# Attention on one core: adaLN columns spread over all its units, VectorE in written order, and a head group's sum of squares taken two units later

## The chip, the core and the metric

The kernel runs on one core of a Trainium2 chip. The metric is device time in microseconds (us) of one execution. The engines are TensorE (PE, with its weight loads PEld), VectorE (DVE), ScalarE (ACT), GpSimd (POOL) and SyncE (SP), which issues the loads from HBM.

## What is computed

One encoder layer on 256 tokens of width 2048, all in float32: a gated feed-forward half step, sixteen heads of attention, and a second half step. Nine vectors of the vector `c` (adaLN: shift, scale and gate of each of the three parts) modulate it.

```python
mod = jax.nn.silu(c) @ w_ada[l] + b_ada[l]
sh1, sc1, gt1, sh2, sc2, gt2, sh3, sc3, gt3 = jnp.split(mod, N_MOD, axis=-1)
f = swiglu(modulate(rms_norm(h, g_ffn1[l]), sh1, sc1), w1_gate[l], w1_up[l], w1_down[l])
h = h + 0.5 * gt1[:, None, :] * f
nrm = modulate(rms_norm(h, g_mix[l]), sh2, sc2)
qkv = nrm @ w_qkv[l]
...
o_na = rms_norm(o_na.reshape(B, S, D_NA), g_out_na[l])
o_dil = rms_norm(o_dil.reshape(B, S, D_DIL), g_out_dil[l])
mix = jnp.concatenate([o_na, o_dil], axis=-1) @ w_o[l]
h = h + gt2[:, None, :] * mix
f = swiglu(modulate(rms_norm(h, g_ffn2[l]), sh3, sc3), w2_gate[l], w2_up[l], w2_down[l])
h = h + 0.5 * gt3[:, None, :] * f
```

Heads 0 to 7 (neighbourhood attention) and heads 8 to 15 (dilated attention) each have a norm of their own over the eight heads' outputs, `o_na` and `o_dil`: that is where a head group's sum of squares is needed.

## The kernel before

**Weights as a stream.** All weights come in chunks of 128 x 1024 float32 (512 KB), loaded by SP into five `raw` buffers (`rw`). Each chunk is split in two: ACT casts it to a rounded `hiw` (L144), DVE subtracts to get the rest, `low` (L147). PE multiplies with both. There are `LOB = 4` buffers of each half, and chunks are prepared `AHEAD = 3` chunks ahead, so the cast for chunk u + 4 refills the buffer that the matmuls of chunk u read.

**Units and slots.** In attention one chunk is one *unit*: 96 of them make q, k and v (four groups of heads, 24 units each, eight units for each of v, k and q; L606 and L609), and 32 more, units 96 to 127, make the output projection (L643 and L648; 16 for heads 0 to 7, then 16 for heads 8 to 15). `at(u, fn)` puts small work into *slot* u, which the program writes behind unit u's matmuls. The heads' attention goes into the slots of the units that follow their q, k and v, by the table `PLAN`: transposes of q and k (`pT`) and their split (`th`, `tl`); scores (`psc`), bias and maximum (`sc`, `mx`), exponential, reciprocal and scaling (`sm`, `sc`); transposes of the weights (`pP`) and their split (`ph`, `pl`); the product with v (`po`), and last `d_ew`: ACT and DVE write both halves of the head's output (`ox`), ACT squares `po` (`sq`, L193), and DVE adds the square to the group's sum (`sqa`, L183). With the eighth head, PE adds up over partitions with two matmuls against ones (`pstat`, L206 and L207), in that head's own slot. From `pstat` comes `rsr`, which every unit of the output projection needs in its update `fin`, one slot after its matmuls: an ACT copy `wt`, and on DVE L632, L633 and L634, which adds to the residual `h`. In the second half the update's square goes to a further sum for the next norm.

**adaLN columns.** A column of `w_ada` is 1 MB (`ra`), reduced against `c` by one DVE instruction and its accumulator read (both L127). Columns that are not due yet are taken from a list `bg` at a rate: each chunk prepared earns `ws.rate` of a column. In attention the list holds the 22 columns of the next feed-forward part (vectors 6 and 7).

**What sets the order.** Every engine runs its list from the front. A scheduler makes the lists, except for engines under `manual_schedule`, which keep the written order. Through units 8 to 121 that is PE alone (`MANUAL`); ahead of that and behind it PE and DVE (`STARTUP`). `keep_in_program_order` (the set `pinned`) holds single instructions in written order.

Of the kernel before, what the change touches and what calls it, by code (L numbers as in the profile page):

```python
# [12 lines left out]
ALU = mybir.AluOpType  # L13
# [3 lines left out]
S = 256  # L17
D = 2048
KT = D // P
# [15 lines left out]
TAIL = 6  # L35
# [5 lines left out]
RA = 0.475  # L41
RB = 0.33
RBD = 0.45
RQ = 0.35
RF = 0.1
AHEAD = 3
RAWB = 5
ARA = 2
ARX = 1
LOB = 4  # L50
MANUAL = {mybir.EngineType.PE}
STARTUP = {mybir.EngineType.PE, mybir.EngineType.DVE}
# [12 lines left out]
def build(tc, a):  # L65
    nc = tc.nc
    with ExitStack() as ctx:
# [17 lines left out]
        def bank(nm):  # L85
            return pools["p"].tile([P, 512], F32, tag="b", name=nm)
# [3 lines left out]
        ones = cp.tile([P, P], F32, name="ones")  # L90
# [83 lines left out]
        class Stat:  # L174
# [11 lines left out]
            def add(self, t, last_dve=True, late=False):  # L186
                self.fold()
                sq = sp.tile([P, S], F32, tag="sq", name="sq")
                self.n += 1
                if self.n == self.total and last_dve:  # L190
                    nc.vector.tensor_tensor(sq, t, t, ALU.mult)
                else:
                    nc.scalar.activation(sq, t, AF.Square)  # L193
                n, total = self.n, self.total
                if n == 1:
                    self.first = sq
                elif n == 2:
                    self.acc = sp.tile([P, S], F32, tag="sqa", bufs=1, name="sqa")
                    nc.vector.tensor_tensor(self.acc, self.first, sq, ALU.add)
                elif n < total:  # L200
                    self.late = sq
                    if not late:
                        self.fold()
                else:
                    self.ps = bank("pstat")[:, :S]
                    nc.tensor.matmul(self.ps, ones, self.acc, start=True, stop=False)  # L206
                    nc.tensor.matmul(self.ps, ones, sq, start=False, stop=True)  # L207

            def rstd(self, n, tag="rs"):
                return rstd_from(self.ps, n, S, tag)  # L210

        def norm_pair(ks, r, jsh, jsc):

            sh, gs = mods[jsh], mods[jsc]
            ts = []
            for k in ks:
                ts.append(sp.tile([P, S], F32, tag="nt", name="nt"))
                nc.vector.scalar_tensor_tensor(ts[-1], h[k], gs[:, k : k + 1], r, ALU.mult, ALU.mult)
                nc.scalar.activation(nx[k][:, 0, :], ts[-1], AF.Identity, bias=sh[:, k : k + 1])  # L219
            for k, t in zip(ks, ts):  # L220
                nc.vector.scalar_tensor_tensor(  # L221
                    nx[k][:, 1, :], t, sh[:, k : k + 1], nx[k][:, 0, :].bitcast(F32), ALU.add, ALU.subtract)
# [13 lines left out]
        pinned = set()  # L236

        def bg_add(ids, then=None):

            ids = list(ids)  # L240
            bg.extend((i, then if i == ids[-1] else None) for i in ids)
# [17 lines left out]
        def bg_until(left):  # L259

            while len(bg) + len(pend) > left:
                if bg:
                    bg_step()
                else:
                    bg_use()
# [194 lines left out]
        for q in range(4):  # L460
            for i in range(2):
                sq = hp.tile([P, 2, S], F32, tag="hid", name="sq1")
# [13 lines left out]
        with tc.manual_schedule(engines=STARTUP):  # L476
# [3 lines left out]
            for k in range(K1):  # L480
                ws.fetch(2 * k + 2)
                bg_until((KT - 1 - k) * 2)
                for j in range(2):
                    w = ws.whole()
                    for b in range(8):
                        f, q = 4 * j + b // 2, b % 2
                        nc.tensor.matmul(pa[f][:, q, :], w[:, b * P : (b + 1) * P], full[k],
                                         start=k == 0 and q == 0, stop=k == K1 - 1 and q == 1,
# [41 lines left out]
        with tc.tile_pool(name="att", bufs=2) as ap_, tc.tile_pool(name="atc", bufs=1) as ac:  # L530
# [16 lines left out]
            ost = [Stat(8), Stat(8)]  # L547
# [6 lines left out]
            def at(u, fn):  # L554
                slots.setdefault(u, []).append(fn)
# [97 lines left out]
            def head(g, i, a0, b0, c0, d0):  # L653
                hd = g * 4 + i
# [61 lines left out]
                def d_ew():  # L716
                    po = s_["po"]
                    go = vec[:, GO + hd : GO + hd + 1]
                    nc.scalar.activation(ox[hd][:, 0, :], po, AF.Copy, scale=go)
                    nc.vector.scalar_tensor_tensor(  # L720
                        ox[hd][:, 1, :], po, go, ox[hd][:, 0, :].bitcast(F32), ALU.mult, ALU.subtract)
                    ost[hd // 8].add(po, False)

                def fetch():
                    s_["bias"] = na_bias(hd) if g < 2 else lnc

                at(max(0, a0 - 2), fetch)
                for u, fn in ((a0, a_pe), (a0 + 1, a_ew), (b0, b_pe), (b0 + 1, b_ew1), (b0 + 2, b_ew2),
                              (c0, c_pe), (c0 + 1, c_ew), (d0, d_pe), (d0 + (0 if d0 == LAST else 1), d_ew)):
                    at(u, fn)  # L730

            last = [j * KT + k for k in range(K2, KT) for j in (7, 6)]
            pinned.update(last[:ARA + 1])
            bg_add(last)
            units = []
            for g in range(4):
# [4 lines left out]
            LAST = len(units) + KT - 1  # L741
            END = len(units) + 2 * KT - 1
# [3 lines left out]
            def run(us):  # L746
                for u in us:
                    if u % 24 == 0 and u <= 72:
                        plan = PLAN if u < 72 else PLAN_L
                        for i in range(4):  # L750
                            head(u // 24, i, *(u + 24 + x for x in plan[i]))
                    if u == END - 2 * TAIL:
                        bg_until(0)
                    units[u](*ws.chunk())
                    if u < 7:
                        norm_pair((2 * u + 2, 2 * u + 3), r2, 3, 4)
                    for f in slots.pop(u, []):
                        f()

            run(range(8))  # L760
            order.close()
            ws.pace(RQ)
            with tc.manual_schedule(engines=MANUAL):
                run(range(8, END - TAIL))
            order.enter_context(tc.manual_schedule(engines=STARTUP))
            run(range(END - TAIL, len(units)))
            for u in sorted(slots):
                for f in slots[u]:
# [5 lines left out]
            last = [8 * KT + k for k in range(KT)]  # L774
# [113 lines left out]
def _program():  # L888
    import concourse.bacc as _bacc

    nc = _bacc.Bacc("TRN2", target_bir_lowering=False, num_devices=1, dynamic_dma_scratch_size=1024)
    aps = {k: nc.dram_tensor(f"in_{k}_dram", s, F32, kind="ExternalInput").ap() for k, s in _SHAPES.items()}
    aps["out"] = nc.dram_tensor("out_0_dram", (KT, P, S), F32, kind="ExternalOutput").ap()
    with tile.TileContext(nc) as tc:
        build(tc, aps)
    return nc
# [10 lines left out]
```

## Time and profile before

| | us |
|---|---|
| median of 3 runs (1944.61 to 1949.75) | 1945.46 |
| the profiled execution | 1942.14 |
| its span, first to last instruction | 1940.4 |
| mean granted PE clock | 0.994 |
| first q/k/v matmul to first output-projection matmul | 782.5 to 1083.6 |
| last output-projection matmul to first matmul of the next part | 1189.1 to 1198.0 |

The profile is of one execution. "Busy" is the time in which an engine works; a wait names the engine and the line whose end released it. The clock is given as a share of full speed. Attention takes about 415 us of the span; what stands ahead of it and behind it is not touched by the change.

### The profile page before, as it was taken

Reading aid. Unit: us, or ns where it says so; the run is one execution under the profiler, and the core shown is the slowest. Engines: PE = TensorE matmul, PEld = TensorE weight load, DVE = VectorE, ACT = ScalarE, POOL = GpSimd, SP = SyncE. Lnnn points to the kernel's source line nnn. Section 1 sums busy time; section 2 is a strip of 40 time slices with the busy share of each in tenths; the row PEclk is TensorE's granted clock in tenths of the full one; section 3 lists DMA queues with packets and bytes.
Section 4 is the critical chain, followed back from the end, with each engine's and each line's share of the span. In section 5 each row is a group of like instructions: output and inputs, shape, how many; then the busy total and the mean of one; then the engine's idle time right before and its main releaser. Section 6 shows DMA issues by size and latency. Waiting matters only on the chain.

```text
span 1940.4 us, 27380 instructions
## 1 busy us (share of the span) xinstructions
PE 1899.4 (98%) x10504; PEld 1648.6 (85%) x10504; DVE 1523.3 (79%) x2055; ACT 907.5 (47%) x1332; POOL 0.7 (0%) x6
## 2 busy tenths in 40 slices
PE   7999999999999999899999998999999999999999
PEld 6878888888888888688888887888888888888888
DVE  7898999999878889699986898668865555555665
ACT  2444544443334454445555565544444433334442
POOL 0000000000000000000000000000000000000000
PEclk9999999999999999999999999999999999999999
DMA  9998888899989898598865544668865666666664
GB/s 392 386 340 303 315 305 309 305 329 395 356 302 345 310 321 311 171 326 324 318 222 165 163 142 146 192 213 318 323 206 186 188 190 186 190 189 187 191 194 134
DMA packets 120083, 503.98 MB, mean 260 GB/s; under 512 B 13328, under 2 KB 15632, under 8 KB 101520
## 3 DMA queue, kind: packets, MB, share of 16 engines
q1 hardware_dynamic: 119952, 502.24, 74.5%
q8 instruction: 82, 1.34, 0.3%
q14 instruction: 49, 0.40, 0.1%
HBM read 500.09 MB, written 2.10 MB: 259 GB/s over the span
## 4 chain that ended last, share of the span: by engine, by line
PE 53%; DVE 4%; issue 1%; ACT 1%; DMA 0%; SPq 0%; ACTq 0%; DVEq 0%
PE pb L338 17%; PE pb L340 9%; PE pd L338 8%; PE pd L340 4%; PE pqq L606 3%; PE pqk L606 3%; PE pqv L606 3%; DVE low L147 2%; PE pqq L609 1%; PE pqk L609 1%; PE pqv L609 1%; PE pso L643 1%; DVE wt L633 1%; PE psc L153 0%; PE po L153 0%
## 5 line engine op out<-in xcount | busy, mean ns | idle before, releaser
L144 ACT CAST hiw<-rw 128x1024 fp32r<-128x1024 f32 x644 | 675.0, 1051 | 793.8 <-PE pd L338 233.7
L147 DVE TENSOR_TENSOR low<-rw,hiw 128x1024 fp32r<-128x1024 f32 x644 | 783.4, 1221 | 293.9 <-ACT hiw L144 286.8
L338 PE MATMUL pb<-nx,hiw 128*128 128x512 f32 x2432 | 610.5, 393 | 4.1 <-DVE nx L221 4.1
L338 PEld LDWEIGHTS pb<-nx,hiw 128*128 128x128 f32 x2432 | 438.4, 189 | 83.0 <-issue 4.4
L340 PEld LDWEIGHTS pb<-nx,low 128*128 128x128 f32 x2432 | 331.7, 190 | 24.5 <-DVE low L147 0.8
L338 PE MATMUL pd<-hd,hiw 128*128 128x512 f32 x1384 | 346.7, 392 | 0.0
L340 PE MATMUL pb<-nx,low 128*128 128x256 f32 x2432 | 339.2, 282 | 0.4 <-DVE low L147 0.4
L338 PEld LDWEIGHTS pd<-hd,hiw 128*128 128x128 f32 x1384 | 248.9, 189 | 44.4
L127 DVE CUSTOM_DVE_ANT_0 ra<-ra,cb,vec 128x2048 f32<-128x2048 f32 x109 | 255.7, 2346 | 11.4 <-DMA ra<-in_w_ada_dram 11.3
L340 PEld LDWEIGHTS pd<-hd,low 128*128 128x128 f32 x1408 | 191.7, 190 | 13.6 <-DVE low L147 0.3
L340 PE MATMUL pd<-hd,low 128*128 128x256 f32 x1408 | 196.5, 282 | 0.0
L402 DVE SCALAR_TENSOR_TENSOR h<-pd,m,h 128x256 f32<-128x256 f32 x126 | 59.5, 481 | 59.4 <-PE pd L340 59.0
L127 DVE CUSTOM_DVE_ANT_0 rx<-rx,cb,vec 128x2048 f32<-128x2048 f32 x35 | 82.1, 2346 | 2.1 <-DMA rx<-in_w_ada_dram 2.1
L338 PE MATMUL pa<-nx,hiw 128*128 128x512 f32 x288 | 72.6, 394 | 6.2 <-ACT hiw L144 6.2
L606 PE MATMUL pqv<-hiw,nx 128*128 128x512 f32 x256 | 66.7, 403 | 5.4 <-ACT nx L219 5.4
L338 PEld LDWEIGHTS pa<-nx,hiw 128*128 128x128 f32 x288 | 51.7, 189 | 16.7 <-ACT hiw L144 7.4
L606 PE MATMUL pqk<-hiw,nx 128*128 128x512 f32 x256 | 65.4, 396 | 0.3 <-ACT hiw L144 0.3
L606 PE MATMUL pqq<-hiw,nx 128*128 128x512 f32 x256 | 64.6, 394 | 0.0
L643 PE MATMUL pso<-ox,hiw 128*128 128x512 f32 x248 | 64.2, 402 | 0.0
L606 PEld LDWEIGHTS pqv<-hiw,nx 128*128 128x128 f32 x256 | 48.3, 193 | 17.8 <-ACT nx L219 7.9
L606 PEld LDWEIGHTS pqk<-hiw,nx 128*128 128x128 f32 x256 | 46.4, 188 | 9.5 <-ACT hiw L144 0.7
L606 PEld LDWEIGHTS pqq<-hiw,nx 128*128 128x128 f32 x256 | 46.8, 188 | 9.1
(143 smaller groups left out, 1370.9 us busy)
## 6 DMA issues: line engine op xcount, KB each, us to landing
ra<-in_w_ada_dram SPq DMA_DIRECT2D x109, 1024.0 KB, 7.3
rw<-in_w_b_dram SPq DMA_DIRECT2D x200, 512.0 KB, 4.4
rw<-in_w_d_dram SPq DMA_DIRECT2D x128, 512.0 KB, 4.3
rw<-in_w_c_dram SPq DMA_DIRECT2D x96, 512.0 KB, 3.6
rw<-in_w_qkv_dram SPq DMA_DIRECT2D x96, 512.0 KB, 4.4
rx<-in_w_ada_dram SPq DMA_DIRECT2D x35, 1024.0 KB, 7.1
rw<-in_w_e_dram SPq DMA_DIRECT2D x48, 512.0 KB, 4.6
rw<-in_w_a_dram SPq DMA_DIRECT2D x44, 512.0 KB, 5.3
```

The lines of the kernel that those rows point to most:

```text
L127: dot = nc.vector.tensor_tensor_reduce(out=raw, in0=raw, in1=cb, scale=1.0, scalar=vec[:, BA + i : BA + i + 1], op0=ALU.mult, op1=ALU.add, ...
L144: cast = nc.scalar.copy(hi, raw)
L147: nc.vector.tensor_tensor(lo, raw, hi.bitcast(F32), ALU.subtract)
L338: nc.tensor.matmul(out, w, r, start=first, stop=False)
L340: nc.tensor.matmul(out[:, :S], lo[:, b * P : (b + 1) * P], r[:, 0, :], start=False, stop=last)
L402: nc.vector.scalar_tensor_tensor(h[d], part_, gate(d), h[d], ALU.mult, ALU.add)
L606: nc.tensor.matmul(ps[t], nx[k][:, i, t * P : (t + 1) * P], whi[:, kk * 512 : (kk + 1) * 512], start=k + i == 0, stop=False)
L609: nc.tensor.matmul(ps[t], nx[k][:, 0, t * P : (t + 1) * P], wlo[:, kk * 512 : (kk + 1) * 512], start=False, stop=k == KT - 1)
L633: nc.vector.scalar_tensor_tensor(t, t if u < END else ps[:, :S], gt2[:, d : d + 1], rows[b], ALU.mult, ALU.mult)
L643: nc.tensor.matmul(ps, w, o, start=kk == 0, stop=False)
```

## The change

Five edits, four of them in attention. `RQ`, the rate of the columns in attention, goes from 0.35 to 0.26 of a column a chunk. All 22 columns are pinned, not the first three. DVE joins PE under written order in units 8 to 121. What is left of the columns is used up at unit 95 (`LAST - KT`, ahead of the output projection) and not at unit 115. For the two head groups (`last_dve` false) the last square is added on DVE like the others (L209), and PE's total is one matmul, in a new function `total_up`, two units after the eighth head's `po`.

```diff
-RQ = 0.35
+RQ = 0.26
...
-                else:
+                elif last_dve:
                     self.ps = bank("pstat")[:, :S]
                     nc.tensor.matmul(self.ps, ones, self.acc, start=True, stop=False)
                     nc.tensor.matmul(self.ps, ones, sq, start=False, stop=True)
+                else:
+                    nc.vector.tensor_tensor(self.acc, self.acc, sq, ALU.add)
+
+            def total_up(self):
+                self.ps = bank("pstat")[:, :S]
+                nc.tensor.matmul(self.ps, ones, self.acc, start=True, stop=True)
...
                     ost[hd // 8].add(po, False)
+                    if hd % 8 == 7:
+                        at(d0 + 2, ost[hd // 8].total_up)
...
-            pinned.update(last[:ARA + 1])
+            pinned.update(last)
...
-                    if u == END - 2 * TAIL:
+                    if u == LAST - KT:
                         bg_until(0)
...
-            with tc.manual_schedule(engines=MANUAL):
+            with tc.manual_schedule(engines=STARTUP):
                 run(range(8, END - TAIL))
```

**What moves: ACT, units 109 to 111.** Heads 12 to 15 finish here. `sq_10517` is the square of head 13, `hiw_10593` (before: `hiw_10595`) the cast of the chunk for unit 115, and `pso_10456` and `pso_10498` are units 109 and 110. Before:

```order
L719 ACTIVATE ox13_7103<-po_10473,vec_76 128x256
L631 COPY wt_10532<-pso_10456 128x256
L144 CAST hiw_10539<-rw_10537 128x1024
L719 ACTIVATE ox14_7104<-po_10520,vec_76 128x256
L156 CAST ph_10565<-pP_10527 128x512
L631 COPY wt_10583<-pso_10498 128x256
L193 ACTIVATE sq_10517<-po_10473 128x256
L144 CAST hiw_10595<-rw_10593 128x1024
```

The same place on ACT after the change, begun a little earlier, with the cast for unit 113 (`hiw_10494`) and head 12's square (`sq_10426`):

```order
L144 CAST hiw_10494<-rw_10492 128x1024
L193 ACTIVATE sq_10426<-po_10374 128x256
L725 ACTIVATE ox13_7103<-po_10473,vec_76 128x256
L690 ACTIVATE sc_10438,sm_10442<-sc_10438,mx_10440 128x256 x2
L144 CAST hiw_10539<-rw_10537 128x1024
L637 COPY wt_10532<-pso_10456 128x256
L725 ACTIVATE ox14_7104<-po_10520,vec_76 128x256
L156 CAST ph_10565<-pP_10527 128x512
L637 COPY wt_10581<-pso_10498 128x256
L144 CAST hiw_10593<-rw_10591 128x1024
L193 ACTIVATE sq_10517<-po_10473 128x256
```

Head 13's square has moved from ahead of the cast for unit 115 to behind it, and head 12's stands behind the cast for unit 113. ACT's order is the scheduler's in both kernels.

**DVE, the same place.** `pl_10566` is the rest of head 15's weights, which PE's `po` of head 15 needs. Before:

```order
L720 SCALAR_TENSOR_TENSOR ox13_7103<-po_10473,vec_76,ox13_7103 128x256
L632 TENSOR_TENSOR wt_10532<-wt_10532,pso_10456 128x256
L147 TENSOR_TENSOR low_10540<-rw_10537,hiw_10539 128x1024
L183 TENSOR_TENSOR sqa_9651<-sqa_9651,sq_10517 128x256
L633 SCALAR_TENSOR_TENSOR wt_10532<-wt_10532,m5_83,rsr_9972 128x256
L720 SCALAR_TENSOR_TENSOR ox14_7104<-po_10520,vec_76,ox14_7104 128x256
L634 TENSOR_TENSOR h3_93<-h3_93,wt_10532 128x256
L157 TENSOR_TENSOR pl_10566<-pP_10527,ph_10565 128x512
L183 TENSOR_TENSOR sqa_9651<-sqa_9651,sq_10562 128x256
```

After, DVE:

```order
L726 SCALAR_TENSOR_TENSOR ox13_7103<-po_10473,vec_76,ox13_7103 128x256
L183 TENSOR_TENSOR sqa_9646<-sqa_9646,sq_10517 128x256
L638 TENSOR_TENSOR wt_10532<-wt_10532,pso_10456 128x256
L639 SCALAR_TENSOR_TENSOR wt_10532<-wt_10532,m5_83,rsr_9972 128x256
L640 TENSOR_TENSOR h3_93<-h3_93,wt_10532 128x256
L147 TENSOR_TENSOR low_10540<-rw_10537,hiw_10539 128x1024
L726 SCALAR_TENSOR_TENSOR ox14_7104<-po_10520,vec_76,ox14_7104 128x256
L183 TENSOR_TENSOR sqa_9646<-sqa_9646,sq_10562 128x256
L157 TENSOR_TENSOR pl_10566<-pP_10527,ph_10565 128x512
```

The addition of head 13's square stands right behind `ox13` now, ahead of the update of unit 109 and the split for unit 114, and head 14's stands ahead of `pl_10566` instead of behind it.

**DVE and ACT, unit 44.** `ox2` belongs to head 2; `sm_8280` and `sc_8276` (before: `sm_8291`, `sc_8287`) are head 3's weights, which PE transposes (`pP`) behind unit 45. DVE before:

```order
L720 SCALAR_TENSOR_TENSOR ox2_7092<-po_8280,vec_76,ox2_7092 128x256
L690 RECIPROCAL sm_8291<-sm_8291 128x2
L127 ISA ra107_8406,m6_84<-ra107_8406,cb_98,vec_76 128x2048
L127 ISA m6_84 128x1
L183 TENSOR_TENSOR sqa_8161<-sqa_8161,sq_8319 128x256
L695 TENSOR_SCALAR sc_8287<-sc_8287,sm_8291 128x256 x2
```

DVE after:

```order
L726 SCALAR_TENSOR_TENSOR ox2_7092<-po_8269,vec_76,ox2_7092 128x256
L183 TENSOR_TENSOR sqa_8151<-sqa_8151,sq_8308 128x256
L696 RECIPROCAL sm_8280<-sm_8280 128x2
L701 TENSOR_SCALAR sc_8276<-sc_8276,sm_8280 128x256 x2
L147 TENSOR_TENSOR low_8317<-rw_8314,hiw_8316 128x1024
```

ACT after, where `hiw_8339` is the cast for unit 49:

```order
L725 ACTIVATE ox2_7092<-po_8269,vec_76 128x256
L144 CAST hiw_8316<-rw_8314 128x1024
L690 ACTIVATE sc_8276,sm_8280<-sc_8276,mx_8278 128x256 x2
L144 CAST hiw_8339<-rw_8337 128x1024
L193 ACTIVATE sq_8308<-po_8269 128x256
```

The column that stood between `sm` and `sc` is gone from this place, `sqa` has moved ahead of both, and head 2's square stands behind the cast for unit 49.

On SP the loads of the columns stand behind every fourth chunk's load instead of every second or third, the last three among those of the output projection. On PE nothing moves but `pstat`.

## The prediction

> **What bounds the kernel now.** I read the busy shares first, then the chain that ended last, then what TensorE (PE) waited for inside attention (770 to 1200 us), and the stages last. The page gives busy time by engine, and the chain's shares:
>
> ```profile
> PE 1899.4 (98%) x10504; PEld 1648.6 (85%) x10504; DVE 1523.3 (79%) x2055; ACT 907.5 (47%) x1332; POOL 0.7 (0%) x6
> ...
> PE 53%; DVE 4%; issue 1%; ACT 1%; DMA 0%; SPq 0%; ACTq 0%; DVEq 0%
> ```
>
> PE is the bound; all it does not fill is 41 us. Its waits in attention (total us, times, longest) show what an edit there can touch:
>
> ```profile
> PE pb L338 <- DVE nx L221: 4.1, 1, 4.1
> PE pstat L206 <- DVE sqa L183: 2.9, 1, 2.9
> PE pT L663 <- DVE qn L589: 2.0, 1, 2.0
> PE pP L701 <- DVE sc L695: 1.5, 2, 0.8
> PE po L153 <- DVE pl L157: 1.2, 1, 1.2
> ...
> PE pstat L207 <- ACT sq L193: 1.1, 1, 1.1
> PE pT L663 <- DVE qn L574: 0.6, 1, 0.6
> ```
>
> The first two rows belong to the norm behind attention, which keeps its place. The other five make 6.4 us, nearly all waits for VectorE (DVE). The stages show why; columns are PE, PEld, DVE, ACT and POOL busy, clock, DMA share, GB/s, and the last row counts L127 alone:
>
> ```profile
> 850.00:900.00 50.00, 50.00 (x239) 41.61 (x238) 49.31 (x70) 26.29 (x52) 0.00 (x0) 1.00 0.90 341
> ...
> 1000.00:1050.00 50.00, 50.00 (x242) 41.72 (x241) 33.24 (x58) 26.82 (x53) 0.00 (x0) 1.00 0.55 169
> ...
> 1100.00:1150.00 50.00, 47.69 (x287) 42.23 (x288) 47.17 (x96) 29.23 (x60) 0.00 (x0) 0.97 0.45 141
> 782.50:1085.00 302.50, 51.77 (x44) 0.99 0.72 251
> ```
>
> DVE is full at 850, has 16.8 us in 50 free at 1000, and is full again in the first output-projection units. A column is two L127 instructions, so 22 columns cost 51.77 us, 2.35 each, all before 1000.
>
> **The columns at an even pace.** Nothing is added: the same 22 columns, one in four units instead of three. Units are 302.5 / 96 = 3.15 us, so about four columns (10 us of DVE) leave the full stretch for the free one. Their loads move on SP's queue, three of them among the output weights; a load has about 12 us until its use, against 7.3 to landing:
>
> ```profile
> ra<-in_w_ada_dram SPq DMA_DIRECT2D x109, 1024.0 KB, 7.3
> ```
>
> So I cost the loads at nothing; if that cover were gone, DVE would stand for the difference, with every split behind it. The two pP waits and the qn wait of 0.6 should go: **-2.1** (0 to -2.1). In the last head group, which had no column, two now fall within five units together with the rope norms: 4.7 us against the idle of five units, 16.8 / 50 x 15.7 = 5.3, not all of it in the right place. I take **+2.0** for pP at unit 93, between 0 (idle suffices) and 3.
>
> **Written order, the part that decides.** DVE works its list from the front, and an addition of squares (sqa) waits for ACT's square (sq), which waits for DVE's ox. In the order shown ahead, ACT's sq of head 13 now stands behind the cast `hiw_10593`, and sqa stands on DVE ahead of a head's update, split and pl. That cast refills the buffer that unit 111's matmuls read, so it cannot start before they end. What each link takes, around the same place before (PE, then ACT, then DVE):
>
> ```profile
> 1137.80 1.07 PE L648 MATMUL pso<-ox,low 128*128 128x256 f32 x8
> ...
> 1140.23 0.39 PE L153 MATMUL po<-pl,vh 128*128 128x256 f32 x1 [1.25 <-DVE pl L157]
> ...
> 1142.59 0.80 PE L207 MATMUL pstat<-sq,ones 128*128 128x256 f32 x2 [1.07 <-ACT sq L193]
> ```
>
> ```profile
> 1137.99 1.05 ACT L144 CAST hiw<-rw 128x1024 fp32r<-128x1024 f32 x1 [0.65 <-PE pso L643]
> 1139.33 0.38 ACT L193 ACTIVATE sq<-po 128x256 f32<-128x256 f32 x1 [0.29 <-DVE ox L720]
> ```
>
> ```profile
> 1138.76 0.48 DVE L720 SCALAR_TENSOR_TENSOR ox<-po,vec,ox 128x256 fp32r<-128x256 f32 x1
> ...
> 1139.48 0.69 DVE L157 TENSOR_TENSOR pl<-pP,ph 128x512 fp32r<-128x512 f32 x1
> ```
>
> The cast starts 0.19 us after the first low matmul of its unit, and PE came to the po that needs pl at 1140.23 - 1.25, which is 1.18 after that same start. One cycle of unit updates with sqa right behind h, on DVE, and PE beside it:
>
> ```profile
> 1173.80 1.22 DVE L147 TENSOR_TENSOR low<-rw,hiw 128x1024 fp32r<-128x1024 f32 x1
> 1174.94 0.42 DVE L632 TENSOR_TENSOR wt<-wt,pso 128x256 f32<-128x256 f32 x1
> ...
> 1175.91 0.43 DVE L634 TENSOR_TENSOR h<-h,wt 128x256 f32<-128x256 f32 x1
> 1176.88 0.43 DVE L183 TENSOR_TENSOR sqa<-sqa,sq 128x256 f32<-128x256 f32 x1 [0.54 <-ACT sq L193]
> 1177.22 1.22 DVE L147 TENSOR_TENSOR low<-rw,hiw 128x1024 fp32r<-128x1024 f32 x1
> ```
>
> ```profile
> 1175.06 2.00 PE L643 MATMUL pso<-ox,hiw 128*128 128x512 f32 x8
> 1176.90 1.07 PE L648 MATMUL pso<-ox,low 128*128 128x256 f32 x8
> 1177.80 0.39 PE L643 MATMUL pso<-ox,hiw 128*128 128x512 f32 x1
> ```
>
> So an update (wt to h) takes 1.40, a split 1.14 until the next, and the cycle 3.42 where PE needs 2.74.
>
> - **po of head 15 (unit 111):** from the first low matmul: cast done 1.24, sq of head 13 1.67, its sqa 2.12, update of unit 109 3.5, split 4.65, ox of head 14 5.1, its sq 5.55, its sqa 6.0, pl 6.65. PE stands from 1.18, 5.4 us in place of 1.25: **+4.1** (down to 2, were DVE through with the update and split by other means).
> - **po of head 13 (unit 109):** sq of head 12 stands behind the cast that waits for unit 109; 1.24, sq 1.67, sqa 2.12, pl 2.8, less 1.18: **+1.6** (0 to 1.6).
> - **pP of head 3 (unit 45):** the same knot: the sq of head 2 behind the cast that waits for unit 45, and sm and sc of head 3 behind sqa. Such links before, on DVE and PE:
>
> ```profile
> 973.22 0.42 DVE L183 TENSOR_TENSOR sqa<-sqa,sq 128x256 f32<-128x256 f32 x1
> 973.56 0.16 DVE L690 RECIPROCAL sm<-sm 128x2 f32<-128x2 f32 x1
> ...
> 974.22 0.61 DVE L695 TENSOR_SCALAR sc<-sc,sm 128x256 f32<-128x256 f32 x2
> ```
>
> ```profile
> 972.76 1.08 PE L609 MATMUL pqk<-low,nx 128*128 128x512 f32 x4
> 974.62 0.70 PE L701 MATMUL pP<-ident,sc 128*128 128x128 f32 x4 [0.78 <-DVE sc L695]
> ```
>
>   1.67 for cast and sq, 0.42 + 0.16 + 0.61 behind it, less the 1.08 that PE still works: **+1.7** (0 to 1.8).
> - **pT of head 12 (unit 100)** waited 2.0 with DVE's list already re-sorted around ACT's rsr; written order adds the idle for it: **+1.0** (-2.0 to 2.5).
> - **Lag between those places:** DVE had 2.8 us free in 50 at 1100 and is blocked twice for about 1 us: psc of head 15 and po of head 14 come late by **+2.0** together (0 to 3).
>
> **The sums of squares two units later.** One matmul of two goes, and PE no longer stands at 1142.59 (1.1). What is late next is rsr, for which all updates of the second half queue. Rows from DVE (first and fifteenth update, the norm's first product) and PE (the total before that product):
>
> ```profile
> 1148.97 0.41 DVE L632 TENSOR_TENSOR wt<-wt,pso 128x256 f32<-128x256 f32 x1
> ...
> 1189.49 0.42 DVE L632 TENSOR_TENSOR wt<-wt,pso 128x256 f32<-128x256 f32 x1
> ...
> 1196.29 0.88 DVE L218 SCALAR_TENSOR_TENSOR nt<-h,m,rsr 128x256 f32<-128x256 f32 x2
> ```
>
> ```profile
> 1193.22 0.70 PE L207 MATMUL pstat<-sq,ones 128*128 128x256 f32 x2 [0.55 <-DVE sq L191]
> ```
>
> Before, the first update came 8.0 us after PE was done with po (1140.93, its 1140.23 and six short matmuls). Now: two units of 2.74, the total, and 3.1 from a total to the first product that uses it, 8.7: +0.7. Then 14 updates took 40.5, 2.89 each; about five more of them now have sqa right behind h, at 3.42: +2.7. The norm starts behind the last update, so both arrive at the end: **+3.4** (-2 to 6); the removed wait is inside it.
>
> **The clock.** Behind the two short gaps at 1139 and 1142 the granted clock fell to half:
>
> ```profile
> 1142.00:1144.00 2.00, 1.41 (x4) 1.16 (x5) 2.00 (x5) 0.92 (x3) 0.00 (x0) 0.77 0.00 0
> 1144.00:1146.00 2.00, 2.00 (x6) 1.57 (x5) 1.84 (x5) 0.35 (x1) 0.00 (x0) 0.50 0.46 113
> ```
>
> That cost PE 0.23 x 2 + 0.5 x 2 and some more, about 1.7, hidden in the 8.0 above. A gap of 5.4 will bring at least the same, and now it delays the total: **+1.7** (0 to 3.4). The Trainium skill (TensorE: Matmul & The Clock Gate, "What's actually happening") says that the clock halves after an idle window of about 3.4 us. This trace differs: its gaps were 1.25 and 1.07. By the page the old drop should not be there, and the new gap alone would earn one; its sum would be 1.7 higher than a sum without a drop, as mine is.
>
> **Sum:** -2.1 + 2.0 + 4.1 + 1.6 + 1.7 + 1.0 + 2.0 + 3.4 + 1.7 = +15.4 us. The profiled execution took 1942.1 (span 1940.4), so 1957.5; the median of the runs shown lies 3.3 higher, which gives 1960.9. I say 1960.
>
> **Rivals.**
> 1. *The waits simply go (faster).* Even DVE load removes pP, qn, pT, po and pstat, 6.4, and the half clock, 1.7: -8.1, 1934 to 1937. For it: every one is a wait for DVE (or its square) where DVE is full. Against: it decides when ACT makes each square before the next unit's cast, and in ACT's list four of them (units 44, 92, 108, 110) stand behind it. Chance 0.04.
> 2. *Blocks, but mostly hidden.* The three knots cost 7.4, but the lag terms, the late rsr and the clock give nothing, and -2.1 - 1.1 are gained: +4, 1946 to 1950. For it: PE waits at the norm anyway, so lag there may be absorbed. Chance 0.13.
> 3. *DVE becomes the bound of all 32 projection units.* At 3.42 against 2.74 it falls behind 0.68 a unit; splits are three units ahead, 8.2 us, so from the twelfth unit on PE waits for low itself: the other 20 cost 13.6 in place of the 5.4 of lag and late rsr in the sum, +23.6, 1966 to 1969. Against: only about half the units have that order. Chance 0.13.
> 4. *Forecast*, 1951 to 1967: chance 0.70.
>
> **How the numbers follow.** A measurement here tells 0.3% (5.8 us) from no change. Faster by more: rival 1, 0.04. Within: nearly all of rival 2, 0.11. Slower: 0.85. The range 1948 to 1972 holds the forecast, the upper half of rival 2 and rival 3.
>
> **What would show it.** In the new profile: po waits for pl of about 5 us at unit 111 and 1.6 at unit 109; pP waits in the first and third group; DVE idle before sqa, released by ACT sq, of several us; cycles of 3.4 us on DVE behind the total; 11 to 13 us (9.0 before) from the last pso matmul to pb; clock at half behind the 5 us gap. No row of pstat waiting for a head's square. It would be wrong if ACT's squares were done before DVE asks for them, if po's longest wait stayed near 1.2, or if the norm started as early after unit 127 as before.

## The result, and the profile after

| | before | after |
|---|---|---|
| median | 1945.46 us (1944.5 to 1949.75, 5 runs) | 1963.98 us (1962.98 to 1964.93, 5 runs) |
| span of the profiled execution | 1940.4 us | 1961.2 us |
| TensorE busy | 1899.4 us | 1905.4 us |

The ratio is 1.0094, with a 95% interval from 1.0081 to 1.0107: slower by 0.9%. The medians differ by 18.5 us, the two profiled spans by 20.8 us; the accounts below are made against the spans.

First what TensorE waited for between 770 and 1225 us in the changed kernel (total us, times, longest):

```profile
PE pstat L206 <- DVE sqa L183: 9.3, 1, 9.3
PE po L153 <- DVE pl L157: 7.3, 3, 5.2
PE pP L707 <- DVE sc L701: 5.4, 2, 3.9
...
PE pT L669 <- DVE qn L595: 2.9, 1, 2.9
```

The same rows named 2.9, 1.2, 1.5 and 2.0 before (`qn` is the normed q that pT transposes). TensorE is still the busiest engine, with 97% of the span; what has grown is its waits, and those that grew are all for VectorE. The timeline of TensorE shows where each is (start, duration, what, and in brackets the idle time ahead of it). Before, at the places that had not been shown:

```profile
1076.99 0.60 PE L701 MATMUL pP<-ident,sc 128*128 128x128 f32 x4
...
1099.94 0.33 PE L663 MATMUL pT<-ident,qn 128*128 128x128 f32 x1 [2.02 <-DVE qn L589]
...
1192.00 0.67 PE L206 MATMUL pstat<-sqa,ones 128*128 128x256 f32 x2 [2.93 <-DVE sqa L183]
```

After:

```profile
925.04 0.63 PE L707 MATMUL pP<-ident,sc 128*128 128x128 f32 x4 [1.57 <-DVE sc L701]
...
1079.99 1.09 PE L707 MATMUL pP<-ident,sc 128*128 128x128 f32 x4 [3.86 <-DVE sc L701]
...
1106.40 0.48 PE L669 MATMUL pT<-ident,qn 128*128 128x128 f32 x1 [2.86 <-DVE qn L595]
...
1140.96 0.39 PE L153 MATMUL po<-pl,vh 128*128 128x256 f32 x1 [1.42 <-DVE pl L157]
...
1145.33 0.39 PE L153 MATMUL po<-pl,vh 128*128 128x256 f32 x1 [0.65 <-DVE pl L157]
...
1154.73 0.58 PE L153 MATMUL po<-pl,vh 128*128 128x256 f32 x1 [5.20 <-DVE pl L157]
...
1212.17 1.19 PE L206 MATMUL pstat<-sqa,ones 128*128 128x256 f32 x2 [9.35 <-DVE sqa L183]
```

These are pP at units 45 and 93, pT of head 12, po of heads 13, 14 and 15, and the total of the norm. The lateness against before can be read along the rows: pP at unit 93 is 1079.99 - 1076.99 = 3.0 us late, pT 6.5, po of head 15 (1140.23 before) 14.5, the norm's total 20.2. Waits alone do not give this. Between pP at unit 93 and pT the lateness grows by 3.5, of which the longer wait for qn is 0.8. The rest is the clock. In these windows of 0.1 us of the changed kernel the third number from the end is the granted clock:

```profile
1078.60:1078.70 0.10, 0.00 (x0) 0.00 (x0) 0.00 (x0) 0.10 (x1) 0.00 (x0) 1.00 0.11 41
1078.70:1078.80 0.10, 0.00 (x0) 0.00 (x0) 0.00 (x0) 0.10 (x1) 0.00 (x0) 0.53 0.02 0
1085.40:1085.50 0.10, 0.10 (x1) 0.08 (x1) 0.00 (x0) 0.10 (x1) 0.00 (x0) 0.50 0.91 369
1085.60:1085.70 0.10, 0.10 (x2) 0.10 (x1) 0.00 (x0) 0.02 (x1) 0.00 (x0) 1.00 0.42 164
```

From 1078.7 to 1085.5 the clock is half, and TensorE works in that stretch from 1079.99 on: 5.5 us at half rate, 2.8 lost. Windows of the same kind find two more half stretches in attention, 1106.0 to 1109.4 (TensorE works in it from 1106.4, behind pT) and 1153.8 to 1160.6 (from 1154.7, behind po of head 15), with 1.5 and 3.0 lost. Before there was one, 1143.1 to 1146.5, with 1.7 lost. Two more are in both kernels and outside this count: at the start of attention (781.3 to 788.0 before, 781.8 to 788.5 after) and behind the wait ahead of the norm (1194.3 to 1201.1 before, 1205.0 to 1222.1 after).

So the 20.8 us are: waits in attention 15.6 in place of 6.5 (+9.1); half clock 7.3 in place of 1.7 (+5.6); the wait ahead of the norm 9.35 in place of 2.93 + 0.55 (+5.9); together 20.6. Smaller items of either sign are left out, among them the norm's two totals, which take 1.0 us longer at half clock; that the sum comes so near is in part luck.

### The profile page after: what moved, and what is told of

The parts are those of the page before. It is cut to its first block, busy times and chain, and to the rows that moved or that the text cites. A ratio compares the mean times of both kernels' runs of the same rounds, so it can differ in the third digit from the quotient of the medians.

```text
span 1961.2 us, 27376 instructions
## 1 busy us (share of the span) xinstructions
PE 1905.4 (97%) x10500; PEld 1653.0 (84%) x10500; DVE 1530.9 (78%) x2057; ACT 907.3 (46%) x1332; POOL 0.7 (0%) x6
## 4 chain that ended last, share of the span: by engine, by line
PE 56%; DVE 2%; ACT 1%; issue 0%; ACTq 0%
PE pb L344 17%; PE pb L346 9%; PE pd L344 8%; PE pd L346 4%; PE pqk L612 3%; PE pqq L612 3%; PE pqv L612 3%; PE pso L649 2%; PE pqk L615 1%; PE pqq L615 1%; PE pqv L615 1%; PE pso L654 1%; DVE low L147 1%; PE psc L153 1%; PE po L153 1%
## 5 line engine op out<-in xcount | busy, mean ns | idle before, releaser
L346 PEld LDWEIGHTS pb<-nx,low 128*128 128x128 f32 x2432 | 331.8, 190 | 24.5 <-DVE low L147 0.8
```

Source lines behind the costliest of these rows:

```text
L346: nc.tensor.matmul(out[:, :S], lo[:, b * P : (b + 1) * P], r[:, 0, :], start=False, stop=last)
```

## The experiments

All times are compared with runs of the kernel before on the same chip; each ratio is to those, with its 95% interval. The medians of before in these series lie between 1945.46 and 1946.32, so where an edited kernel is set beside the changed kernel (1963.98), a difference of about 1 us tells nothing. Two words are used. A **knot** is a square of a head (ACT, L193) that stands in ScalarE's list behind a cast of weights that must wait for TensorE, with a VectorE addition (sqa) that waits for the square. The **place** of an instruction is where it stands in VectorE's written list, wanted or not.

### Each part alone, and the written order undone

Columns alone (label e1_cols), on the kernel before:

```diff
-RQ = 0.35
+RQ = 0.26
-            pinned.update(last[:ARA + 1])
+            pinned.update(last)
-                    if u == END - 2 * TAIL:
+                    if u == LAST - KT:
```

> The kernel before with the columns' edit alone (all 22 pinned, RQ 0.26, the stage's columns drained at unit 95); VectorE keeps its re-sorted list and the head's squares their place. Theory of the knots (what costs is VectorE standing in written order behind an addition of squares): nothing to lose here, the two pP waits and the qn wait of the first two groups (2.1 us) go, 1942 to 1946. Rival 'late columns crowd the last head group': the pP wait of 3.9 us at unit 93 and the half clock behind it stay, 1949 to 1953.

Written order alone (e2_order):

```diff
-            with tc.manual_schedule(engines=MANUAL):
+            with tc.manual_schedule(engines=STARTUP):
```

> The kernel before with VectorE in written order in units 8 to 121 alone; columns early and squares as before. Theory of the knots: po waits of 1.4 and 5 us at units 109 and 111, pT about 2.5, half clock behind them, the norm some 5 us late; no column stands ahead of ox at unit 93, so no wait near 3.9 us there: +11 to +15, 1956 to 1961. Rival 'late columns': within 4 of before, 1942 to 1950. Rival 'VectorE short of throughput in all 32 output units': waits of PE for low (L147) in the units behind the twelfth, over 1964.

The later total alone (e3_squares): the edits to Stat.add, total_up and d_ew, with the rest as before.

> The kernel before with the third edit alone: the last square of eight added on VectorE, one total two units later. Theory of the knots: pstat's wait of 1.07 us and the half clock behind it go, the updates start about 0.7 us later: 1943 to 1948. Rival 'the later total makes rsr and with it the norm late': the wait ahead of the norm grows by the two units, 5 us, 1949 to 1952.

The changed kernel with the written order taken back (e5_undo_order): the line of e2_order reversed.

> The changed kernel with VectorE's list re-sorted again in units 8 to 121; even columns and the later total stay. Theory of the place (in written order VectorE comes to what TensorE asks for only behind everything written ahead of it): the waits at units 45, 109 and 111 fall to before's, unit 93 keeps about 3 us because the column stands there, 1942 to 1947. Rival 'even columns and the later total are the cost': over 1954.

| kernel | median us | ratio to before |
|---|---|---|
| columns alone | 1944.72 | 0.9994 (0.9985 to 1.0002) |
| written order alone | 1965.39 | 1.0095 (1.0081 to 1.0109) |
| later total alone | 1944.07 | 0.9988 (0.9978 to 0.9999) |
| columns and later total | 1947.56 | 1.0005 (0.9994 to 1.0015) |

The written order is the whole loss, shown from both sides: alone it costs as much as the whole change, and without it the loss is gone. The other two edits are worth nothing that can be told, or 0.1%. The later total alone did take pstat's wait for the square away, and the half clock behind it, as expected; but in the re-sorted list the waits for sc grew from 1.5 to 3.1 us and those for qn at 947 us from 0.6 to 1.8. Together and re-sorted the two edits keep a wait of 2.9 us at unit 93, as expected, and have a new one of 2.2 for qn at 1022.6.

Two things in this group were expected wrongly. The written order alone was to cost 11 to 15 us without a wait near 3.9 at unit 93; it cost 19, and the wait had moved to another unit. Its waits for sc, in attention:

```profile
PE pP L701 <- DVE sc L695: 5.3, 2, 3.8
```

The longest of the two, 3.8, stands at unit 69, where a column still stands ahead of ox; at unit 93, where the columns have ended, there is none. In the changed kernel it is the other way round, and VectorE's rows at unit 93 have the column right ahead of ox, the square's addition and sc:

```profile
1075.56 2.35 DVE L127 CUSTOM_DVE_ANT_0 ra<-ra,cb,vec 128x2048 f32<-128x2048 f32 x1
...
1078.03 0.48 DVE L726 SCALAR_TENSOR_TENSOR ox<-po,vec,ox 128x256 fp32r<-128x256 f32 x1
1078.96 0.42 DVE L183 TENSOR_TENSOR sqa<-sqa,sq 128x256 f32<-128x256 f32 x1 [0.45 <-ACT sq L193]
```

So the 3.8 us go with the column. And the columns alone, without written order, were to lose the pP waits; they lost those of before and got one of 2.9 us at unit 93, with a half stretch behind it, which is why the even pace gains nothing. The waits for sc with the columns alone:

```profile
PE pP L701 <- DVE sc L695: 2.9, 1, 2.9
```

### What stands ahead of sc: a knot, or a column

Columns kept out of units 1 to 3 and 17 to 21 of each 24, still in written order (e14_written_gaps):

```diff
-RQ = 0.26
+RQ = 0.42
+                    if u >= 8:
+                        ws.rate = 0.0 if u > 92 or u % 24 in (1, 2, 3, 17, 18, 19, 20, 21) else RQ
                     units[u](*ws.chunk())
```

> The changed kernel, still in written order, with the same 22 columns kept out of the units in which rope norms and a head's softmax end meet (units 1 to 3 and 17 to 21 of each 24, none behind 92; RQ 0.42 in the others). Theory of the place: no column stands ahead of ox at unit 93, so pP's wait of 3.9 us falls under 1.5 and the half clock behind it goes, 5 to 7 us, 1957 to 1960. Rival 'VectorE is short of throughput in attention': denser columns elsewhere make new waits of the same sum, 1962 to 1966.

It took 1961.94 us, 1.0083 (1.0070 to 1.0097): 2 us less than the changed kernel, where 5 to 7 were expected, and at the edge of the rival's range. The 3.9 did fall, to 1.53, and the half clock behind it went. But there are now four waits for sc, of 1.53, 1.56, 1.53 and 1.53 us, at units 45, 65, 69 and 93:

```profile
PE pP L707 <- DVE sc L701: 6.2, 4, 1.6
```

This is what a knot costs, and the changed kernel itself shows it with and without. At unit 45, ScalarE and then VectorE:

```profile
922.65 1.05 ACT L144 CAST hiw<-rw 128x1024 fp32r<-128x1024 f32 x1 [0.71 <-ACT sc L690]
923.60 0.38 ACT L193 ACTIVATE sq<-po 128x256 f32<-128x256 f32 x1
```

```profile
921.72 0.48 DVE L726 SCALAR_TENSOR_TENSOR ox<-po,vec,ox 128x256 fp32r<-128x256 f32 x1
924.01 0.42 DVE L183 TENSOR_TENSOR sqa<-sqa,sq 128x256 f32<-128x256 f32 x1 [1.81 <-ACT sq L193]
```

At unit 69:

```profile
998.90 0.38 ACT L193 ACTIVATE sq<-po 128x256 f32<-128x256 f32 x1 [1.07 <-DVE ox L726]
999.54 1.05 ACT L144 CAST hiw<-rw 128x1024 fp32r<-128x1024 f32 x1 [0.26 <-PE pqq L612]
```

```profile
998.39 0.48 DVE L726 SCALAR_TENSOR_TENSOR ox<-po,vec,ox 128x256 fp32r<-128x256 f32 x1
999.32 0.42 DVE L183 TENSOR_TENSOR sqa<-sqa,sq 128x256 f32<-128x256 f32 x1 [0.45 <-ACT sq L193]
```

The view puts the cast's 0.71 us down to ScalarE's own sc, which ended at 921.94; the cast starts 0.25 us after TensorE's first matmul on that unit's `low` (922.40), so what it waited for is TensorE. Where the cast stands first, VectorE stops 1.81 us at sqa, and TensorE waits 1.57 for the sc behind it. Where the square stands first, VectorE stops 0.45, and TensorE does not wait. In e14_written_gaps all four places where TensorE waits for sc have the square right behind a cast in ScalarE's list, and VectorE stops 0.95 to 1.42 us there. Two more knots in the units of q, k and v (VectorE stops 1.21 us at 1014 and 1.87 at 1064 us) do not make TensorE wait. The knots therefore are real, but here a knot cost TensorE time only where it soon asked for what stands behind it; and the new waits, 6.2 us in all in place of 5.4, come as the rival had them in sum, but not from denser columns. At unit 93 of the changed kernel the cost was another one, the column of 2.35 us shown above, which stands ahead of ox, so that the square was asked for late. Taking the columns away there brought knots elsewhere, because ScalarE's list was sorted anew. What one edit frees, the re-sorted engine spends again.

All squares ahead of their casts, by putting ScalarE in written order too (e7_act_too):

```diff
-            with tc.manual_schedule(engines=STARTUP):
+            with tc.manual_schedule(engines=STARTUP | {mybir.EngineType.Activation}):
```

> The changed kernel with ScalarE in written order as well in units 8 to 121, so that no head's square stands behind a later cast of weights. Theory of the knots (square behind cast is what costs): po's wait at unit 109 (1.4) and pP's at unit 45 (1.6) go, the one at 111 falls by about 1, and about 5 us come back, 1957 to 1960. Theory of the place: VectorE is busy ahead of those places anyhow; the waits at 93, 111 and ahead of the norm stay within 0.6 us, 1961 to 1966.

It took 1991.01 us, 1.0232 (1.0217 to 1.0247), 27 more than the changed kernel: a miss of both expectations. What ScalarE itself waits for between 830 and 1230 us (total, times, longest) says why:

```profile
ACT sc L690 <- DVE mx L687: 79.5, 16, 7.6
ACT sq L193 <- DVE ox L726: 31.3, 16, 4.0
```

ScalarE now stands before each exponential until VectorE has the row maxima, and the casts that would have filled that time stand behind it. VectorE in turn waits 51.9 us for casts (`low <- hiw`) in place of 24.5. With two engines in written order each waits for the other's turn. No square stands behind a later cast any more, yet VectorE still stands 8.9 us at sqa for squares (11.8 in the changed kernel), and something worse is there; as a measure of the knots alone this run is inconclusive.

Each addition of a square one slot later (e4_fold_later; for the eighth square, directly ahead of the total):

```diff
-                    nc.vector.tensor_tensor(self.acc, self.acc, sq, ALU.add)
+                    self.late = sq
             def total_up(self):
+                self.fold()
-                    ost[hd // 8].add(po, False)
-                    if hd % 8 == 7:
-                        at(d0 + 2, ost[hd // 8].total_up)
+                    ost[hd // 8].add(po, False, late=True)
+                    at(d0 + 2, ost[hd // 8].total_up if hd % 8 == 7 else ost[hd // 8].fold)
```

> The changed kernel, with each addition of a head's square (sqa) written one slot later than its square, so that VectorE does not stand behind a square that has only just been asked for. Theory of the knots: po's wait at unit 111 falls from 5.2 to under 2, the one at unit 109 from 1.4 to under 0.5, pP at unit 93 from 3.9 to about 2.8 (the column ahead of ox stays), the half-clock stretches behind po go, and the norm comes 5 us earlier: 1950 to 1956. Rival 'VectorE short of throughput in written order': no wait changes by more than 1 us, 1961 to 1966.

It took 1962.38 us, 1.0080 (1.0068 to 1.0093), far from the 1950 to 1956 expected. The waits behind knots did go: none at units 45 and 109, 2.8 in place of 5.2 at unit 111, 3.0 at unit 93, as the theory had them. But the edit made two long new ones. The total of the first half now stands right behind its last addition and TensorE waits 3.2 us for it at 1014 us, and pT of head 12 waits 1.4 and then 4.1 us for qn: VectorE stands 2.6 us for squares of the q norm, which ScalarE's list has behind a cast, and an update and a split of weights are written between the two parts of qn. The gain was given back in new waits.

### Head 15: the place of pl, and the clock

In the changed kernel VectorE has these instructions ahead of the pl that TensorE wants from 1149.5 on:

```profile
1149.87 0.43 DVE L183 TENSOR_TENSOR sqa<-sqa,sq 128x256 f32<-128x256 f32 x1 [1.04 <-ACT sq L193]
1150.21 0.41 DVE L638 TENSOR_TENSOR wt<-wt,pso 128x256 f32<-128x256 f32 x1
...
1151.53 1.22 DVE L147 TENSOR_TENSOR low<-rw,hiw 128x1024 fp32r<-128x1024 f32 x1
1152.66 0.48 DVE L726 SCALAR_TENSOR_TENSOR ox<-po,vec,ox 128x256 fp32r<-128x256 f32 x1
1153.65 0.43 DVE L183 TENSOR_TENSOR sqa<-sqa,sq 128x256 f32<-128x256 f32 x1 [0.51 <-ACT sq L193]
1153.99 0.68 DVE L157 TENSOR_TENSOR pl<-pP,ph 128x512 fp32r<-128x512 f32 x1
```

This is the chain that the prediction wrote down link by link. Only the first idle time in it, 1.04, has to do with a knot; update, split, ox and the second sqa are work that nobody waits for yet. To test that, pl alone is written a slot earlier (e12_pl_earlier):

```diff
-                              (c0, c_pe), (c0 + 1, c_ew), (d0, d_pe), (d0 + (0 if d0 == LAST else 1), d_ew)):
+                              (c0, c_pe), (c0 + (1 if d0 > c0 + 1 else 0), c_ew), (d0, d_pe), (d0 + (0 if d0 == LAST else 1), d_ew)):
```

> The changed kernel with one split (ph and pl of head 15) written a slot earlier, ahead of one update, one split of weights, one ox and one sqa on VectorE. Theory of the place: po's wait at unit 111 falls from 5.2 to 1 to 2, the half clock behind it goes, the norm comes 5 to 6 us earlier, 1957 to 1960. Theory of the knots: pl still stands behind the sqa of head 13, whose square stands behind the cast, at least 3.5 us of the wait stay, 1961 to 1964.

It took 1960.66 us, 1.0077 (1.0062 to 1.0092), 3.3 less than the changed kernel and between the two ranges; the waits decide between the theories. TensorE around the same place:

```profile
1149.96 0.39 PE L153 MATMUL po<-pl,vh 128*128 128x256 f32 x1 [1.42 <-DVE pl L157]
...
1152.80 0.50 PE L649 MATMUL pso<-ox,hiw 128*128 128x512 f32 x1 [0.59 <-DVE ox L726]
1154.23 0.47 PE L649 MATMUL pso<-ox,hiw 128*128 128x512 f32 x1 [0.92 <-DVE ox L726]
```

The wait fell from 5.2 to 1.42, and the half clock went, as the place has it. Two new waits of 0.6 and 0.9 for ox take their turn, as the work that stood ahead of pl now stands ahead of ox. Of the 5 to 6 us expected, 3.3 came, and of these 0.9 was there ahead of head 13 already, by a chance of the clock (see the last section).

Filling the wait in place of shortening it (e11_fill):

```diff
-                    s_["po"] = bank("po")[:, :S]
+                    b_ = bank("po")
+                    s_["po"] = b_[:, :S]
+                    if hd == NH - 1:
+                        for _ in range(32):
+                            nc.tensor.matmul(b_[:, S:], res[g, "v", 0][0][:, hs], ox[0][:, 0, :], start=True, stop=True)
```

> The changed kernel with 32 matmuls more on TensorE ahead of head 15's po (into the unused half of po's bank, about 0.12 us each, 3.75 us), so that TensorE works through most of its 5.2 us of waiting. If the half clock behind that wait comes from the idle time and delays the total: the wait falls to about 1.4, units 112 and 113 run at full clock, the norm comes about 2 us earlier, 1960 to 1963. Rival 'the half clock is covered by the wait ahead of the norm': no change, 1963 to 1965. Rival 'the added work is paid in full': 1966 to 1969.

It took 1960.80 us, 1.0077 (1.0060 to 1.0094): with 3.75 us of useless matmuls added, 3.2 us less than the changed kernel. The wait ahead of po's pl is 1.44, and the clock behind it stays full, as this window of 2 us has it (the third number from the end):

```profile
1154.00:1156.00 2.00, 2.00 (x12) 1.74 (x13) 0.48 (x1) 0.65 (x2) 0.00 (x0) 1.00 0.42 168
```

Between the profiled executions the norm's total comes 3.5 us earlier (1208.65). Of that 0.9 was there ahead of head 13 already, as the half stretch behind unit 93 cost less; the other 2.6 came behind head 15, though pl itself comes no earlier. The first update behind the total starts at 1163.06 in place of 1166.55, 8.5 us after po is done, for which the prediction had worked out 8.7. So the half clock behind head 15 cost some 2.6 us of its own, on top of the wait, and it is the idle time that brings it. Of the 3.5 us some 1.3 are lost again: the half clock behind the norm lasts 6.0 us from the first product on, 3.4 in the changed kernel, and the profiled spans differ by 2.3.

### The wait ahead of the norm

The norm's squares added one update later in all updates of the second half, not only in the last (e13_hsq_later):

```diff
-                        hst.add(h[d], late=u > END - TAIL)
+                        hst.add(h[d], late=True)
```

> The changed kernel with the norm's squares added one update later in all 16 updates of the second half (before: in the last ones alone), so that no sqa stands right behind its h. If the cycle of update, square and sqa in written order sets the norm's start: the fifteenth update starts some 40 us behind the first in place of 43.1, the wait ahead of the norm falls from 9.3 to about 6.5, 1960 to 1962. Rival 'the late total sets it': the wait stays over 8.5, 1963 to 1965.

It took 1959.89 us, 1.0073 (1.0056 to 1.0090), 4.1 less than the changed kernel, of which the profiled spans show 3.4. Its first and fifteenth updates start at 1166.41 and 1206.50, 40.1 us apart in place of 43.1 (1166.55 to 1209.66), and the wait ahead of the norm is 3 us shorter:

```profile
PE pstat L206 <- DVE sqa L183: 6.3, 1, 6.3
```

The cycle of update, split and sqa in written order, in which VectorE waits for the square in 7 of 14 cycles of the changed kernel (3.7 us in sum; before in 2, with 1.1), makes 3 of the 6.4 us by which the wait ahead of the norm grew. The other 3.4 stay. They lie with the total: the first update still starts 10.5 us behind po of head 15, where it was 8.0, and TensorE, which no longer stands at pstat, comes to the norm 1.3 us sooner. So the rival is wrong as the only cause, but has a part.

### The parts together, and a faster kernel

The mends of e14_written_gaps, e12_pl_earlier and e13_hsq_later at once, in written order (e15_mended):

> The changed kernel, in written order, with three edits at once: columns out of the crowded units, ph and pl of head 15 a slot earlier, the norm's squares added one update later. If the three terms are separate places: 5 to 7, 3 and 3 us come back, 1950 to 1954, still slower than before, since pT at head 12, po at units 109 and 110 and the late first update stay. Rival 'one backlog of VectorE': the second and third overlap, 1954 to 1957.

It took 1955.18 us, 1.0050 (1.0036 to 1.0064). The three alone gave 2.0, 3.3 and 4.1 us, 9.4 together; at once they gave 8.8. The time itself lies in the range of the rival, one backlog. But the sum is nearly kept, and the waits of the single runs are all there again (6.2 for sc, 3.4 for pl, 6.3 ahead of the norm), which speaks for separate places; the sum fell short of what was expected because the first part had been taken at 5 to 7. Mended at three places, written order still loses 0.5%.

The columns out of the crowded units and the later total, with VectorE re-sorted as before (e10_list_gaps; the edit of e14_written_gaps and the line of e2_order reversed):

> The columns out of the crowded units and the later total, with VectorE's list re-sorted as before (no written order in units 8 to 121). Theory of the place: the waits for sc at unit 93 (2.9 with even columns) and for qn go, pstat's stall and its half clock go, what stays is pT at head 12, po at unit 111 and the norm: 1938 to 1943, faster than both. Rival 'the sorter moves the columns anyhow': pP and pT waits of 1 to 3 us elsewhere, 1944 to 1949.

It took 1939.78 us (1938.84 to 1940.58, 6 runs), 0.9969 (0.9958 to 0.9981): faster than both. Its waits:

```profile
PE pstat L206 <- DVE sqa L183: 3.2, 1, 3.2
PE pP L707 <- DVE sc L701: 2.2, 2, 1.2
PE pT L669 <- DVE qn L595: 2.0, 1, 2.0
PE po L153 <- DVE pl L157: 1.2, 1, 1.2
```

The wait of 2.9 us at unit 93 that the even pace has without written order is gone, and there is no pstat stall on a head's square. What remains are two short pP waits and those that before had too. The gain is small, 0.3%, though its interval does not reach 1; which of the two edits brings it was not tested.

## Why the prediction was right, and where it was off

The prediction said +15.4 us on the profiled execution; it was +20.8 there, and +18.5 by the medians. Its terms beside what the rows show:

| term | predicted | measured |
|---|---|---|
| old pP waits and qn gone | -2.1 | -2.1 |
| pP at unit 93 | +2.0 (0 to 3) | +3.9 |
| po of head 15 | +4.1 | +3.95 |
| po of head 13 | +1.6 | +1.4 |
| pP at unit 45 | +1.7 | +1.6 |
| pT of head 12 | +1.0 | +0.8 |
| lag at psc of head 15 and po of head 14 | +2.0 | +0.65 |
| late rsr and updates, removed stall inside | +3.4 | +4.8 |
| half clock (measured: half of TensorE's working time in the half stretches) | +1.7 (0 to 3.4) | +5.6 |

The sum is 5 us short: 3.9 of it the clock, 1.9 pP at unit 93, 1.4 the norm, against 1.35 too much for the lag.

- **Written order decides**: right, and shown by taking it back (e5_undo_order) and by trying it alone (e2_order).
- **The chains at units 45, 109 and 111**: right within 0.2 us each. As to their cause the experiments divide them: unit 45 is the knot, unit 111 mostly the place of pl behind work that is not wanted yet (e12_pl_earlier).
- **pP at unit 93**: mis-sized, and by the wrong reason. The prediction took two more columns against the idle of five units, 4.7 against 5.3. The sum over five units was not what counted: the list is worked in order, and one column of 2.35 us stands directly ahead of the ox from which square, sqa and sc follow. Nor is it a matter of written order alone: the even columns cost 2.9 there where VectorE is re-sorted, too (e1_cols).
- **The clock**: the term with the largest error. The prediction gave one half stretch, behind po of head 15. There were three, because waits of 3.9 and 2.9 us at unit 93 and pT bring one each, and two of them lasted 6.8 us in place of 3.4. The prediction also said that this trace differs from the Trainium skill (TensorE: Matmul & The Clock Gate, "What's actually happening"), as gaps of 1.25 and 1.07 us were enough. It does: of the four windows that brought a drop in attention, before and after, three were not idle throughout (1.65, 2.47 and 2.57 us of 3.41). What the prediction missed is that the section also says that the window, 3413 ns long, runs freely. With that the traces agree (51.2 us between two half stretches are 15 windows of 3.41), and so the price of a wait depends on where it falls: see the last section.
- **The norm**: first update 0.7 late by the total, and 2.7 by the cycle; measured 2.6 by the cycle (43.1 against 40.5). The first update came 10.6 us behind po of head 15 (1155.96 to 1166.55) and not 8.7, since the two units in between ran at half clock; at full clock it came at 8.5 (e11_fill). The sign given for the norm, 11 to 13 us from the last output-projection matmul to pb, was passed: 15.9 us, 1202.8 to 1218.7.
- **The loads**: costed at nothing, and rightly: between 830 and 1220 us VectorE waits for no column's load.
- **Rivals**: that the waits simply go was wrong, as they grew from 6.5 to 15.6 us. That the blocks are mostly hidden was wrong too: the late rsr gave 4.8 us and the clock 5.6, where it had nothing. VectorE as the bound of all output units did not happen: TensorE never waited there for low.

## What to carry to other kernels

An engine in written order is as late as everything written ahead of what is wanted: before fixing the order of one engine, walk the list between each waiting instruction and its input and add up what stands there, waits for other engines included. Averages of idle time over some units say nothing about it. Where a wait of some microseconds on TensorE remains, price the half clock behind it as well (here 2.8 us lost behind a wait of 3.9, 1.5 behind 2.9, 3.0 behind 5.2; a wait of 2.9 across an edge of the clock's grid cost none); and where lists of other engines are sorted by a scheduler, look at those lists again after each edit, since a freed place can tie a new knot.

## What was not expected of the hardware

The half clock comes in steps, on a grid. Its starts in the profile of the changed kernel, 1078.7, 1106.0, 1153.8 and 1205.0, lie 27.3, 47.8 and 51.2 us apart, which is 8, 14 and 15 times 3.41; its stretches last 6.8, 3.4, 6.8 and 17 us. In the kernel before:

```profile
1142.90:1143.00 0.10, 0.10 (x3) 0.09 (x1) 0.10 (x1) 0.00 (x0) 0.00 (x0) 1.00 0.00 0
1143.10:1143.20 0.10, 0.10 (x2) 0.02 (x2) 0.10 (x1) 0.00 (x0) 0.00 (x0) 0.50 0.00 0
1146.30:1146.40 0.10, 0.10 (x2) 0.10 (x1) 0.00 (x0) 0.00 (x0) 0.00 (x0) 0.50 0.80 328
1146.50:1146.60 0.10, 0.10 (x2) 0.05 (x2) 0.00 (x0) 0.00 (x0) 0.00 (x0) 1.00 0.70 287
```

The step ahead of 1143.06 began at 1139.65 and had 0.58 us of the first gap (to 1140.23) and 1.07 of the second in it, 1.65 idle. With the columns alone the same two gaps, 1.24 and 1.07, lie at 1141.76 to 1143.00 and 1144.29 to 1145.36, and the clock stays full:

```profile
1142.00:1144.00 2.00, 1.00 (x7) 0.89 (x7) 2.00 (x7) 0.80 (x3) 0.00 (x0) 1.00 0.67 233
1144.00:1146.00 2.00, 0.93 (x5) 0.59 (x4) 1.93 (x5) 0.76 (x2) 0.00 (x0) 1.00 0.06 23
```

On that kernel's grid (a half stretch of it starts at 1078.55; 19 steps of 3.41 later is 1143.4) an edge falls between the gaps. The wait at unit 93 shows the same with more at stake. With the columns alone it is 2.95 us and lies in one step (to 1078.55), and the clock halves. With columns and later total together it is as long, but an edge at 1078.72 (33 steps ahead of a half stretch that begins at 1191.36) parts it into 1.36 and 1.58 us, and the clock stays full:

```profile
1080.30 0.63 PE L707 MATMUL pP<-ident,sc 128*128 128x128 f32 x4 [2.94 <-DVE sc L701]
1078.70:1082.10 3.40, 1.80 (x10) 1.61 (x11) 3.37 (x6) 0.67 (x2) 0.00 (x0) 1.00 0.93 326
```

How much idle time a step must have is not sharp. The wait of 1.57 us at 925 in the changed kernel lies within one step and brought no drop; and in the kernel before the step from 1187.43 to 1190.85 has 1.77 us idle, more than the 1.65 above, and the next step is at full clock:

```profile
1187.40:1190.80 3.40, 1.67 (x15) 1.47 (x13) 3.29 (x7) 0.42 (x1) 0.00 (x0) 1.00 0.70 176
1190.90:1194.20 3.30, 1.37 (x4) 0.59 (x4) 2.70 (x5) 1.59 (x3) 0.00 (x0) 1.00 0.34 139
```

Over the steps between 800 and 1235 us in the profiles of both kernels and all twelve experiments (each with the grid of its own half stretches), each step at full clock with 1.92 us idle or more was followed by half clock, and none with 1.90 or less was, but for the one with 1.65; why that one differs is not shown. Whether gaps meet in one step is chance: in the changed kernel, e12_pl_earlier and e11_fill, which are alike up to head 14, the half clock behind unit 93 begins at 1078.71, 1080.91 and 1081.24 us, and lasts 6.8 us in the first and 3.4 in the other two, 0.9 us of TensorE's time. That the times of one kernel scatter by 3 to 7 us (columns and later total together: 1942.6 to 1949.7) may come from this; that was not tested.
